# One decoder layer on one core: attention steps under a higher priority, the first x pairs on GpSimd's queue, sums tiles kept inside their group

## The chip, the core and the metric

The kernel runs on one core of one Trainium2 chip. The metric is the device time of one launch in microseconds (us). Of the kernel before, three runs took 2105.9, 2107.91 and 2104.35 us, so its median is 2105.9 us.

## What is computed

One layer for 256 tokens of width 2048, all in float32: a gated feed-forward block (f1), a mixing stage, cross-attention to 256 memory rows, a second feed-forward block (f2), a final norm. Cut to what matters:

```
h = x
h = h + 0.5 * swiglu(rmsnorm(h, g_ffn1), w1_gate, w1_up, w1_down)
z = rmsnorm(h, g_mix) @ w_in                      # u, v, q, k, v of the window attention
y_a = gelu(u) * (w_s @ rmsnorm(gelu(v)) + b_s)
y_b = window_attention_sinks(q, k, v, sinks)      # 16 heads of 64, window 128
h = h + concat(rmsnorm(y_a), rmsnorm(y_b)) @ w_out
h = h + cross_attention(rmsnorm(h, g_x), rmsnorm(mem, g_mem), w_xq, w_xkv, w_xo)
h = h + 0.5 * swiglu(rmsnorm(h, g_ffn2), w2_gate, w2_up, w2_down)
out = rmsnorm(h, g_final)
```

## The kernel before

**Products.** Every float32 operand is held as two float32r parts, a high part and what is left of it (names ending in h and l). `split` (L148 on ScalarE: a cast to the high part; L149 on VectorE: the subtraction that gives the low part) makes them from a value in float32, `split_scaled` (L142, L143) does it with a gain. A product is three matmuls: high by high, low by high, high by low (L363). Nearly all of TensorE's time is such 128x512 matmuls.

**Units and chunks.** A unit is a product of all 256 tokens by 1024 columns of a weight matrix, summed in up to seven PSUM banks that are named P, Q, R and so on behind the unit's name. It goes through its weights in chunks of 1 MB (`push`, `load`): the load is issued from SyncE (raw tile, three buffers), ScalarE casts wh, VectorE subtracts wl (two buffers each), TensorE multiplies. Where a chunk has kind S, VectorE also adds up sums of its blocks (t) and both engines split them into th and tl, of which there is one buffer each. In the names, f1gwh is the high part of a chunk of f1's gate and up weights, f1dwh and f1dth those of its down weights, uwh, vwh, mv0wh those of the mixing stage and of the memory's values. The token side of a product is a `Pair`: 256 rows of the transposed operand, split in the same way, plus split sums for kinds C and S. A pair of kind C needs half a tile of sums; two of them share a tile through the list `shared`.

**Order.** TensorE's order is the order of the program. The other engines' orders come from a scheduler, which picks among the instructions by priority (the place in the program; a `tc.high_priority()` block moves its instructions ahead) as dependencies and buffers become free in its own estimate. Once fixed, each engine works through its order one by one and waits at the first instruction that is not ready.

**Start.** The first unit (f1g, kind N) multiplies chunks c0, c1, c2 ... by the pairs n0 of x. The transposed x comes in pairs of 256 KB (n0r, L244, from SyncE's queue; the very first from ScalarE's). Beside it h (that is, x by rows) is loaded in four pieces of 512 KB (L747) and squared on ScalarE (junk, L138) for the norm. From c4 on, transposes of the scaled rows (n, L218) make the pairs n1 of the later units.

**Window attention** (`attend`, L861 and on) runs as side work between the matmuls of the units v, u and mv0, two lanes of it: scores (sc, TensorE), scaled, masked and maximum taken on VectorE (scs, mx, esk, nmx, L889 to L898), exponentials on ScalarE (L900), transposes on TensorE (pT), copied to SBUF by VectorE (pTs, L913), product with the values on TensorE (wop, L918), and the division at the end (esk L924, den L925, yb L928). In the same stretch the rows of memory are scaled into pairs mT for the unit mv0 (mTr L263, mTf, mTfh, mTfl; loads on GpSimd's queue), and ScalarE evacuates the units' banks through Gelu (v L956, u L969).

**Cross-attention** (`attend_memory`) is side work between the matmuls of xq and xo in the same way.

## Time and profile before

| | |
|---|---|
| three timed runs | 2104.35 to 2107.91 us, median 2105.9 us |
| the profiled execution | 2105.79 us by the timer, span 2104.0 us |
| outside the span | 1.79 us |
| TensorE busy | 2076.0 us, 99% of the span |
| VectorE, ScalarE, GpSimd busy | 1674.5, 1135.4, 32.2 us |
| mean granted TensorE clock | 0.996 |
| read from HBM | 398.52 MB, 190 GB/s over the span |

PE is TensorE, DVE VectorE, ACT ScalarE, POOL GpSimd, SP SyncE; PEclk is the clock that TensorE was granted, as a share of full speed. A row of a timeline has the start, the duration, engine, line, operation, output and inputs, and in brackets the idle time ahead of it with what ended it. On DVE and ACT the next instruction begins up to 0.1 us before the former's end in these rows.

### The profile page before, as it was taken

How to read it: one execution, taken by the hardware profiler on the slowest of the kernel's cores; microseconds unless marked ns; L12 is line 12 of the kernel's file. 1: busy time of each engine (PE TensorE's matmuls, PEld its weight loads, DVE VectorE, ACT ScalarE, POOL GpSimd, SP SyncE). 2: the span in 40 equal slices, each digit the busy share in tenths (PEclk: the TensorE clock that was granted, in tenths of full speed). 3: DMA queues.
4: the chain of work that ended last, by engine and by line, in shares of the span. 5: the costliest groups of instructions: out<-in, count | busy, mean ns of one | idle time of the engine just before them, and what ended most of it. 6: DMA issues, size and time to landing. Idle time of an engine off the chain costs nothing.

```text
span 2104.0 us, 23815 instructions
## 1 busy us (share of the span) xinstructions
PE 2076.0 (99%) x9527; PEld 1715.5 (82%) x9527; DVE 1674.5 (80%) x1609; ACT 1135.4 (54%) x1109; POOL 32.2 (2%) x51
## 2 busy tenths in 40 slices
PE   9999999999999999999999999999999999999998
PEld 7888888888888888788888888778888888888886
DVE  5888888888987745867858657798888888889878
ACT  7655555555544645544545455665555545555444
POOL 0000000000000000100000000000000000000000
PEclk9999999999999999999999999999999999999999
DMA  7555555555555554435555543455555555555553
GB/s 281 195 189 213 200 195 184 209 188 199 202 199 206 201 210 166 167 140 200 180 180 184 197 160 140 163 197 200 181 207 197 204 191 200 200 200 200 200 198 122
DMA packets 60110, 402.15 MB, mean 191 GB/s; under 512 B 6864, under 2 KB 8928, under 8 KB 12768
## 3 DMA queue, kind: packets, MB, share of 16 engines
q1 hardware_dynamic: 57280, 393.50, 51.7%
q0 software_dynamic: 2016, 6.30, 0.9%
q8 instruction: 74, 1.21, 0.2%
q10 hardware_dynamic: 704, 0.84, 0.1%
q14 instruction: 36, 0.29, 0.0%
HBM read 398.52 MB, written 2.10 MB: 190 GB/s over the span
## 4 chain that ended last, share of the span: by engine, by line
PE 94%; DVE 3%; ACT 1%; issue 1%; DMA 1%; POOL 0%; SPq 0%; POOLq 0%; DVEq 0%; ACTq 0%
PE f2gQ L363 16%; PE f1gQ L363 15%; PE f1dQ L363 6%; PE f2dQ L363 6%; PE f2gP L363 6%; PE f1gP L363 5%; PE f1dP L363 3%; PE f2dP L363 3%; PE woQ L363 2%; PE xqQ L363 2%; PE f1dR L363 2%; PE f2dR L363 2%; PE xoQ L363 2%; PE mk0Q L363 1%; PE mv1Q L363 1%; PE mv0Q L363 1%
## 5 line engine op out<-in xcount | busy, mean ns | idle before, releaser
L149 DVE TENSOR_TENSOR f1gwl<-f1gw,f1gwh 128x2048 fp32r<-128x2048 f32 (+1 forms) x91 | 185.5, 2043 | 51.6 <-ACT f1gwh L148 51.4
L148 ACT CAST f2gwh<-f2gw 128x1536 fp32r<-128x1536 f32 (+1 forms) x88 | 154.4, 1755 | 133.4 <-PE f2gQ L363 96.6
L148 ACT CAST f1gwh<-f1gw 128x2048 fp32r<-128x2048 f32 (+1 forms) x91 | 156.1, 1716 | 123.5 <-PE f1gQ L363 90.4
L149 DVE TENSOR_TENSOR f2gwl<-f2gw,f2gwh 128x1536 fp32r<-128x1536 f32 (+1 forms) x88 | 183.7, 2088 | 40.3 <-ACT f2gwh L148 40.2
L363 PE MATMUL f2gQ<-f2gwh,n4fh 128*128 128x512 f32 x363 | 141.4, 390 | 0.0
L363 PE MATMUL f2gQ<-f2gwh,n4fl 128*128 128x512 f32 x363 | 141.3, 389 | 0.0
L363 PE MATMUL f1gQ<-f1gwh,n1fh 128*128 128x512 f32 x330 | 128.6, 390 | 0.0
L363 PE MATMUL f1gQ<-f1gwh,n1fl 128*128 128x512 f32 x330 | 128.4, 389 | 0.0
L148 ACT CAST f2dwh<-f2dw 128x2048 fp32r<-128x2048 f32 (+1 forms) x44 | 79.2, 1799 | 91.2 <-PE f2dQ L363 71.2
L148 ACT CAST f1dwh<-f1dw 128x2048 fp32r<-128x2048 f32 (+1 forms) x44 | 79.2, 1799 | 87.9 <-PE f1dQ L363 68.2
L149 DVE TENSOR_TENSOR f2dwl<-f2dw,f2dwh 128x2048 fp32r<-128x2048 f32 (+1 forms) x44 | 94.4, 2145 | 27.0 <-ACT f2dwh L148 24.3
L363 PE MATMUL f2gQ<-f2gwl,n4fh 128*128 128x512 f32 x363 | 115.7, 392 | 0.0
L149 DVE TENSOR_TENSOR f1dwl<-f1dw,f1dwh 128x2048 fp32r<-128x2048 f32 (+1 forms) x44 | 94.3, 2144 | 26.8 <-ACT f1dwh L148 24.2
L363 PE MATMUL f1gQ<-f1gwl,n1fh 128*128 128x512 f32 x330 | 105.1, 392 | 0.0
L149 DVE TENSOR_TENSOR f2gtl<-f2gt,f2gth 128x2048 fp32r<-128x2048 f32 x33 | 75.6, 2292 | 17.0 <-ACT f2gth L148 16.6
L149 DVE TENSOR_TENSOR f1gtl<-f1gt,f1gth 128x2048 fp32r<-128x2048 f32 x30 | 68.8, 2292 | 18.3 <-ACT f1gth L148 18.0
L363 PEld LDWEIGHTS f2gQ<-f2gwh,n4fl 128*128 128x128 f32 x363 | 68.1, 188 | 14.2
L363 PEld LDWEIGHTS f2gQ<-f2gwh,n4fh 128*128 128x128 f32 x363 | 68.2, 188 | 14.1
L363 PEld LDWEIGHTS f2gQ<-f2gwl,n4fh 128*128 128x128 f32 x363 | 67.3, 188 | 13.5
L148 ACT CAST f2gth<-f2gt 128x2048 fp32r<-128x2048 f32 x33 | 63.1, 1913 | 23.1 <-DVE f2gt L314 18.3
L363 PEld LDWEIGHTS f1gQ<-f1gwh,n1fl 128*128 128x128 f32 x330 | 62.0, 188 | 12.9
L363 PEld LDWEIGHTS f1gQ<-f1gwh,n1fh 128*128 128x128 f32 x330 | 62.0, 188 | 12.8
(703 smaller groups left out, 5715.1 us busy)
## 6 DMA issues: line engine op xcount, KB each, us to landing
f2gw<-in_w_gu SPq DMA_DIRECT2D x88, 1024.0 KB, 4.8
f1gw<-in_w_gu SPq DMA_DIRECT2D x87, 1024.0 KB, 4.8
f1dw<-in_w_down SPq DMA_DIRECT2D x44, 1024.0 KB, 4.8
f2dw<-in_w_down SPq DMA_DIRECT2D x44, 1024.0 KB, 4.8
wow<-in_w_out SPq DMA_DIRECT2D x16, 1024.0 KB, 4.8
xqw<-in_w_xq SPq DMA_DIRECT2D x16, 1024.0 KB, 4.8
xow<-in_w_xo SPq DMA_DIRECT2D x16, 1024.0 KB, 4.8
qw<-in_w_in SPq DMA_DIRECT2D x8, 1024.0 KB, 5.0
```

Of the source, the lines that this page charges most:

```text
L148: nc.scalar.copy(hi, src)
L149: nc.vector.tensor_tensor(lo, src, hi.bitcast(F32), ALU.subtract)
L363: nc.tensor.matmul(self.banks[name], x, y, start=name not in self.begun, stop=self.left[name] == 0)
```

## The change

Three edits. First, in both attentions, steps on ScalarE and VectorE go under `tc.high_priority()`: in the window attention the mask, maximum and exponentials, the copy pTs and the division; in cross-attention the splits of the transposed queries, of the transposed probabilities and of the output, and the softmax. Second, the loads of the pairs of x (seven, 256 KB each) are issued by GpSimd instead of SyncE. Third, `shared` is emptied between groups of pairs (before mT and before n4), so that a C pair of mT does not take the other half of a sums tile that n1 opened, and one of n4 not that of mT.

```diff
-            nc.sync.dma_start(raw, srcT[i * T:(i + 1) * T, :].rearrange("(k p) t -> p k t", p=P))
+            nc.gpsimd.dma_start(raw, srcT[i * T:(i + 1) * T, :].rearrange("(k p) t -> p k t", p=P))
...
     mT = []
+    shared.clear()
...
-                sc = s2("scs")
...
-                nc.vector.scalar_tensor_tensor(
-                    out=sv, in0=pv, scalar=0.125, in1=bnd, op0=ALU.mult, op1=ALU.add
-                )
...
+                with tc.high_priority():
+                    sc = s2("scs")
...
+                    nc.vector.scalar_tensor_tensor(
+                        out=sv, in0=pv, scalar=0.125, in1=bnd, op0=ALU.mult, op1=ALU.add
+                    )
...
-                pts = s2("pTs")
-                nc.vector.tensor_copy(pts, pt)
+                with tc.high_priority():
+                    pts = s2("pTs")
+                    nc.vector.tensor_copy(pts, pt)
...
-            nc.scalar.activation(esk, esk, AF.Exp)
-            nc.vector.tensor_tensor(den, den, esk, ALU.add)
-            nc.vector.reciprocal(den, den)
...
+            with tc.high_priority():
+                nc.scalar.activation(esk, esk, AF.Exp)
+                nc.vector.tensor_tensor(den, den, esk, ALU.add)
+                nc.vector.reciprocal(den, den)
...
-            split(qh[:, 2 * half:2 * half + 2, :], ql[:, 2 * half:2 * half + 2, :], pv)
+            with tc.high_priority():
+                split(qh[:, 2 * half:2 * half + 2, :], ql[:, 2 * half:2 * half + 2, :], pv)
...
-        split(ph, pl, ptv)
+        with tc.high_priority():
+            split(ph, pl, ptv)
...
+    shared.clear()
     n4, on4, rs4_ = next_norm("n4", G_FFN2, KINDS)
```

TensorE's order of instructions is the same in both programs. The other engines' orders differ at five stretches. In the first feed-forward block's first unit, ScalarE and VectorE both change. On ScalarE, n0r_143 is the second pair of x and n0h_122 its high part, for chunk c1, whose cast is f1gwh_150; junk are the squares of h; the rows stand between the casts of c0 and of c2:

```order
 L148 CAST f1gwh_129<-f1gw_128 128x512 x3
-L142 ACTIVATE n0h_122<-n0r_143,sm 128x256 x2
 L148 CAST f1gwh_150<-f1gw_149 128x2048
-L142 ACTIVATE n0h_183<-n0r_185,sm 128x256 x2
 L138 ACTIVATE junk_192,parts_120<-h 128x512
 L138 ACTIVATE junk_194,parts_120<-h 128x512
+L142 ACTIVATE n0h_122<-n0r_143,sm 128x256 x2
+L142 ACTIVATE n0h_183<-n0r_185,sm 128x256 x2
 L138 ACTIVATE junk_197,parts_120<-h 128x512
```

The pair for c1 has moved behind c1's cast and behind two squares of h. On VectorE its low part n0l has likewise moved from ahead of c1's f1gwl to right behind it; and before chunk c5's pair, two more n1fl subtractions stand ahead of the subtraction f1gwl of c6, behind which n0l for c5 stays.

In f1's down projection, near 620 us of the trace, VectorE's order of the low parts has changed. f1dtl_4469 is the low part of a chunk's sums, f1dwl_4515 that of the chunk behind it, the f1afl are low parts of pairs of activations:

```order
 L313 TENSOR_TENSOR f1dt_4467<-f1dt_4467,f1dw_4463 128x512
+L149 TENSOR_TENSOR f1afl_4545<-f1a_3244,f1afh_4544 128x512
+L149 TENSOR_TENSOR f1dwl_4465<-f1dw_4463,f1dwh_4464 128x1536
 L314 TENSOR_TENSOR f1dt_4467<-f1dt_4467,f1dw_4463 128x512
-L149 TENSOR_TENSOR f1dwl_4465<-f1dw_4463,f1dwh_4464 128x1536
-L149 TENSOR_TENSOR f1afl_4545<-f1a_3244,f1afh_4544 128x512
+L149 TENSOR_TENSOR f1afl_4588<-f1a_3244,f1afh_4587 128x512
+L149 TENSOR_TENSOR f1dwl_4515<-f1dw_4513,f1dwh_4514 128x2048
 L149 TENSOR_TENSOR f1dtl_4469<-f1dt_4467,f1dth_4468 128x2048
-L149 TENSOR_TENSOR f1dwl_4515<-f1dw_4513,f1dwh_4514 128x2048
```

The sums' low part now comes behind that of the next chunk and one more f1afl. On ScalarE the casts f1dth and the next chunk's f1dwh have changed places in the same way, and both orders repeat this at the next chunk of kind S, near 630 us.

In the unit u, near 845 us, VectorE's order ahead of one copy pTs is this before (mTf, mTfl and n1fl belong to the memory pairs; n1fl there is a half tile of sums that n1 opened; uwl_6230 is the low part of u's third chunk):

```order
L960 SCALAR_TENSOR_TENSOR v_5731<-v_5731,rs_6103,gv_5729 128x1024
L960 SCALAR_TENSOR_TENSOR v_5732<-v_5732,rs_6103,gv_5729 128x1024
L263 SCALAR_TENSOR_TENSOR mTr_6110<-mTr_6110,sm,by_token 128x2x128 x2
L198 TENSOR_TENSOR mTf_6117<-mTr_6110 128x256
L149 TENSOR_TENSOR uwl_6230<-uw_6228,uwh_6229 128x2048
L149 TENSOR_TENSOR mTfl_6116<-mTr_6110,mTfh_6115 128x512
L149 TENSOR_TENSOR n1fl_632<-mTf_6117,n1fh_631 128x256
L263 SCALAR_TENSOR_TENSOR mTr_6129<-mTr_6129,sm,by_token 128x2x128 x2
L198 TENSOR_TENSOR mTf_6138<-mTr_6129 128x256
L913 COPY pTs_6165<-pT_6160 128x512
```

And this now:

```order
L964 SCALAR_TENSOR_TENSOR v_5731<-v_5731,rs_6103,gv_5729 128x1024
L964 SCALAR_TENSOR_TENSOR v_5732<-v_5732,rs_6103,gv_5729 128x1024
L932 TENSOR_TENSOR yb_5723<-wop_5810,den_5811 128x512
L263 SCALAR_TENSOR_TENSOR mTr_6110<-mTr_6110,sm,by_token 128x2x128 x2
L149 TENSOR_TENSOR uwl_6146<-uw_6144,uwh_6145 128x2048
L198 TENSOR_TENSOR mTf_6119<-mTr_6110 128x256
L149 TENSOR_TENSOR mTfl_6116<-mTr_6110,mTfh_6115 128x512
L149 TENSOR_TENSOR mTfl_6118<-mTf_6119,mTfh_6117 128x256
L149 TENSOR_TENSOR uwl_6230<-uw_6228,uwh_6229 128x2048
L263 SCALAR_TENSOR_TENSOR mTr_6131<-mTr_6131,sm,by_token 128x2x128 x2
L198 TENSOR_TENSOR mTf_6138<-mTr_6131 128x256
L916 COPY pTs_6165<-pT_6160 128x512
```

Behind v's scaling and ahead of pTs there now stand two rows more, the division yb and the low part uwl_6146 of u's second chunk, which stood ahead of v's scaling before; pTs has kept its place in the queue. On ScalarE the exponential of esk has moved ahead of v's Gelu, with one table load for it, and the cast of u's second chunk has moved behind the four squares of v.

Behind the unit u, where mv0 begins (near 895 us), ScalarE's order has an exponential between u's second and third evacuation, and with it two table loads (ACT_TABLE_LOAD) more. In cross-attention the maximum xmx has moved ahead of one subtraction each of the queries' and the keys' split. From there on the orders of all engines are the same.

## The prediction

> **What bounds the kernel now.** The page comes first, for which engine is full; then the windows by stage, for where that engine is not; then the waits of TensorE, for what it misses there.

> ```profile
> span 2104.0 us, 23815 instructions
> PE 2076.0 (99%) x9527; PEld 1715.5 (82%) x9527; DVE 1674.5 (80%) x1609; ACT 1135.4 (54%) x1109; POOL 32.2 (2%) x51
> ```

> TensorE is idle for 2104.0 - 2076.0 = 28.0 us in all, and its order does not change. Below, a window's columns are its length, busy time of PE, PEld, DVE, ACT and POOL, granted clock, DMA share and GB/s.

> ```profile
> 0.00:62.00 62.00, 57.25 (x247) 45.28 (x248) 38.06 (x54) 46.60 (x81) 2.97 (x12) 0.97 0.75 269
> 820.00:860.00 40.00, 35.43 (x159) 28.63 (x158) 26.10 (x42) 24.28 (x46) 6.51 (x9) 0.91 0.37 132
> ```
> ```profile
> 36.00:46.00 10.00, 7.54 (x30) 5.66 (x28) 6.98 (x11) 5.40 (x10) 0.00 (x0) 0.83 0.81 286
> 845.00:858.00 13.00, 8.43 (x27) 6.25 (x26) 9.96 (x20) 5.08 (x12) 2.88 (x4) 0.74 0.36 121
> ```
> ```profile
> PE wop L918 <- DVE pTs L913: 4.8, 2, 4.6
> ```

> The start and the attention near 850 us hold 4.75 + 4.57 = 9.3 us of the idle time, and the clock falls in both: 10 x (1 - 0.83) = 1.7 us of full speed are lost in one, 13 x (1 - 0.74) = 3.4 us in the other. What this change can win lies there, about 14 us; anything that makes TensorE wait elsewhere is lost in full, since TensorE has no other work.

> **The start, x from GpSimd's queue: +1.1 us.** Chunk c1 began so:

> ```profile
> 11.91 1.91 ACT L148 CAST f1gwh<-f1gw 128x2048 fp32r<-128x2048 f32 x1 [1.66 <-DMA f1gw<-in_w_gu]
> 13.72 0.90 ACT L142 ACTIVATE n0h<-n0r,sm 128x256 fp32r<-128x256 f32 x2
> 14.53 0.62 ACT L138 ACTIVATE junk<-h 128x512 f32<-128x512 f32 x1
> ```
> ```profile
> 13.85 2.29 DVE L149 TENSOR_TENSOR f1gwl<-f1gw,f1gwh 128x2048 fp32r<-128x2048 f32 x1 [3.07 <-ACT f1gwh L148]
> ```
> ```profile
> 13.87 0.50 PE L363 MATMUL f1gP<-f1gwh,n0h 128*128 128x512 f32 x1 [0.62 <-ACT f1gwh L148]
> ...
> 14.68 0.40 PE L363 MATMUL f1gP<-f1gwh,n0l 128*128 128x512 f32 x1
> ...
> 19.86 0.50 PE L363 MATMUL f1gP<-f1gwh,n0h 128*128 128x512 f32 x1 [0.22 <-ACT f1gwh L148]
> ...
> 25.86 0.50 PE L363 MATMUL f1gP<-f1gwh,n0h 128*128 128x512 f32 x1 [0.25 <-ACT f1gwh L148]
> ```
> ```profile
> 5.30 1.71 SPq L747 DMA_DIRECT2D h<-in_x  x2
> ```
> ```profile
> h<-in_x SPq DMA_DIRECT2D x1, 512.0 KB, 8.6
> ```

> c1's pair was ready before its weights. Now ScalarE first squares two pieces of h, and the first h, issued at 5.30, lands 8.6 us later, at 13.9 (the last row is that one load). So: two squares of 0.62 to 15.1; n0h's halves, 0.45 each (row of 13.72), at 15.6 and 16.0; VectorE, through with f1gwl at 16.1, makes n0l's halves by 16.5. c1's fourth matmul moves from 14.68 to some 16.5, by 1.85. The waits of 0.22 and 0.25 us ahead of c2 and c3 (19.86, 25.86) are for weights and absorb 0.47; 1.4 reaches c5.

> c5 waited before, and still does:

> ```profile
> 35.78 0.39 PE L363 MATMUL f1gQ<-f1gwh,n0l 128*128 128x512 f32 x1
> ...
> 38.58 0.50 PE L363 MATMUL f1gP<-f1gwh,n0h 128*128 128x512 f32 x1 [0.59 <-ACT n0h L142]
> 40.95 0.79 PE L363 MATMUL f1gP<-f1gwh,n0l 128*128 128x512 f32 x1 [1.87 <-DVE n0l L143]
> ```
> ```profile
> 38.21 2.29 DVE L149 TENSOR_TENSOR f1gwl<-f1gw,f1gwh 128x2048 fp32r<-128x2048 f32 x1
> 40.41 0.88 DVE L143 SCALAR_TENSOR_TENSOR n0l<-n0r,sm,n0h 128x256 fp32r<-128x256 f32 x2
> ```

> n0l stays behind the subtraction of c6's weights, whose cast needs the buffer that the matmul of 35.78 reads last. That one is 1.4 late, so the cast runs from 37.6 to 39.4, f1gwl to 41.6, n0l's first half to 42.05: 1.1 later than 40.95. From there TensorE runs through as before (c7's pair, earlier than now, was no wait). The start costs +1.1 us, with -0.5 (a piece of h that lands earlier, since two pairs no longer lie ahead of it in its queue) and +2.7 (it lands 1.3 later, below) as ends. The issues themselves cost nothing: GpSimd does little then, and SyncE is relieved of seven.

> ```profile
> n0r<-in_xT SPq DMA_DIRECT2D x6, 256.0 KB, 7.1
> ...
> snk<-in_sinks POOLq DMA_DIRECT2D x1, 8.0 KB, 5.1
> ```

> GpSimd's one load there took 5.1 us for 8 KB, SyncE's pairs 7.1 for 256 KB, so a pair issued near 3.4 lands by about 10.5 at worst, far ahead of 15.1. [...]

> **The sums' order in f1's down projection: +1.8 us.** No intent of the change, only a consequence of tiles that come free at other times.

> ```profile
> 616.99 1.92 ACT L148 CAST f1dth<-f1dt 128x2048 fp32r<-128x2048 f32 x1
> 618.90 1.92 ACT L148 CAST f1dwh<-f1dw 128x2048 fp32r<-128x2048 f32 x1
> ...
> 630.15 1.91 ACT L148 CAST f1dwh<-f1dw 128x2048 fp32r<-128x2048 f32 x1
> ```
> ```profile
> 619.14 2.28 DVE L149 TENSOR_TENSOR f1dtl<-f1dt,f1dth 128x2048 fp32r<-128x2048 f32 x1
> ```
> ```profile
> 618.43 0.39 PE L363 MATMUL f1dQ<-f1dwh,f1afl 128*128 128x512 f32 x1
> ...
> 624.33 1.07 PE L363 MATMUL f1dQ<-f1dtl,f1afh 128*128 128x512 f32 x4
> ...
> 628.63 0.39 PE L363 MATMUL f1dQ<-f1dwh,f1afl 128*128 128x512 f32 x1
> ...
> 634.53 1.07 PE L363 MATMUL f1dQ<-f1dtl,f1afh 128*128 128x512 f32 x4
> ```

> f1dtl was ready at 621.4 and used at 624.33, a margin of 2.9. Now the next chunk's cast goes first. It began at 618.90 right behind f1dth; it writes a buffer that TensorE reads last with the matmul of 618.43 (0.39), so it cannot begin before 618.8, and f1dwl follows from 620.8 to 623.0, f1dtl from 623.0 to 625.25: TensorE waits 0.9 us. The next S chunk, 0.9 late, repeats it: the cast of 630.15 waits for the matmul of 628.63, over at 629.0 + 0.9 = 629.9, and ends at 631.8, f1dth follows to 633.7, VectorE does f1dwl from 631.9 and f1dtl from 634.1 to 636.3; TensorE wants it at 634.53 + 0.95 = 635.5: 0.85 more. Together +1.8; the ends are 0 (the cast finds its buffer free by 2 us more than I count) and 2.3. Near 550 and 560 us the same shuffle leaves margins of over 2.5 us.

> **The urgent steps near 850 us: -0.4 us.**

> ```profile
> 834.79 1.90 ACT L148 CAST uwh<-uw 128x2048 fp32r<-128x2048 f32 x1
> ...
> 837.91 1.28 ACT L924 ACT_TABLE_LOAD   x1
> ```
> ```profile
> 838.94 0.68 DVE L928 TENSOR_TENSOR yb<-wop,den 128x512 f32<-128x512 f32 x1
> ...
> 841.26 2.48 DVE L960 SCALAR_TENSOR_TENSOR v<-v,rs,gv 128x1024 f32<-128x1024 f32 x2 [0.84 <-POOL rs L133]
> ...
> 849.30 0.68 DVE L913 COPY pTs<-pT 128x512 f32<-128x512 f32 x1
> ```

> pTs waits not for its transposes but for its turn: from v's scaling to pTs VectorE is busy without a gap. With the cast of 834.79 (1.8) and the table load of 837.91 (1.28) moved out of the squares' way, v's scaling starts about 3.2 us earlier, at 838.1. But the subtraction uwl (2.2) and yb (0.6) now come behind it and ahead of pTs: 3.2 - 2.8 = 0.4 gained, the wait stays at 4.2 of 4.57, and the low clock with it.

> **At nothing.** The two table loads more near 895 us cost ScalarE 2 x 1.28 and hold up u's third bank; when it was read, and when mv0R wants it:

> ```profile
> 898.43 0.69 ACT L969 ACTIVATE u<-uR,rs 128x512 f32<-128x512 f32 x1 [0.38 <-PE uR L363]
> ```
> ```profile
> 905.24 0.48 PE L363 MATMUL mv0R<-mv0wh,mTfh 128*128 128x512 f32 x1
> ```

> Even 3.5 us later (2 x 1.28 and an exponential with its wait) it is read by 902.7, so 2.5 us of other banks' matmuls cover it; without that cover it would cost up to 3. The steps in cross-attention move by one subtraction or two (0.6 to 1.2 us) where TensorE did not wait, and the sums tiles cost no instruction.

> **The sum** against the profiled execution: 2105.8 + 1.1 + 1.8 - 0.4 = 2108.3 us; that execution lies 0.1 below the median of the three runs, so no correction is due.

> **The rivals.** Slower for good: the squares of h hold c1 for longer. This stage runs its loads so (the second column from the right is the DMA engines' share):

> ```profile
> 12.00:26.00 14.00, 12.92 (x55) 9.71 (x54) 6.66 (x9) 12.35 (x24) 0.73 (x1) 1.00 1.04 403
> ```

> If pairs three and four (512 KB; at 403 GB/s 1.3 us) go ahead of h, n0h starts at 16.4; TensorE then idles near 4 us and the clock falls there as well, by the price of the window at 36 us, 1.7. 2108.3 + 1.3 + 1.7 = 2111.3. It decides from a landing of h later than about 14.8. For it: the pairs no longer wait in SyncE's queue. Against it: their buffers are few.

> The change does what it says at 850 us: pTs comes right behind its transposes, the wait of 4.57 and the 3.4 us of clock go, 2108.3 + 0.4 - 8.0 = 2100.7. Against it stands VectorE's order, in which pTs keeps its place.

> The orders change nothing that TensorE feels: h early, f1dtl in time, pTs 0.4 earlier: 2105.4.

> The clock falls elsewhere. In the trace the low clock follows an idle stretch of 2.4 us near 40 us (1.7 lost) and of 4.6 near 850 (3.4 lost); both stretches move by some tenths. If neither triggers it, 2108.3 - 5.1 = 2103.2. [...]

> **How the numbers follow.** My forecast, 2106.4 to 2110, has 0.45; the slower rival 0.25; no effect 0.12; the clock 0.08; the stall at 850 gone 0.10. A difference of 0.2%, 4.2 us, is about what a measurement of this kernel can tell from none: faster means below 2101.7, slower above 2110.1. Faster: 0.10 and a little of the clock's rival, 0.12. Slower: 0.25 and the forecast's upper edge, 0.27. Same: 0.61. The range, 2102.5 to 2111.8, leaves out the stall's end and the tails.

> **What would show it.** Right: c1's first matmuls wait for ACT n0h and DVE n0l with idle time near 2.5 us; PE f1dQ waits for DVE f1dtl twice in the 620s and 630s, 0.9 us each; wop still waits over 4 us for pTs with the clock near 0.74. Wrong: if wop's wait is gone, the queue's order was not the reason; if f1dQ does not wait, the casts were not held by their buffers; if PE is idle near 895 to 910, the table loads were not covered.

## The result and the profile after

The changed kernel took 2113.0 us (median of 7 runs, 2112.07 to 2114.26), the kernel before 2105.9 (7 runs, 2104.35 to 2107.91): 1.0034 times as long, with a 95% interval of 1.0022 to 1.0045. That is 7.1 us more, where 2.4 were forecast. The profiled execution of after took 2113.46 us, 0.5 above its median; its page begins so:

```profile
span 2111.7 us, 23799 instructions
PE 2078.7 (98%) x9527; PEld 1716.9 (81%) x9527; DVE 1673.5 (79%) x1609; ACT 1138.0 (54%) x1111; POOL 37.2 (2%) x58
```

TensorE is idle for 33.0 us, 5.0 more than before, and busy for 2.7 more with the same matmuls: that part is clock (0.50 for 17.1 us up to 2080 us, in before for 10.2). The windows by stage (length, busy time of PE, PEld, DVE, ACT, POOL, granted clock, DMA share, GB/s), first of after, then of before for the two stages that the prediction does not show:

```profile
0.00:62.00 62.00, 53.89 (x233) 42.96 (x234) 36.41 (x51) 46.20 (x79) 7.96 (x19) 0.94 0.70 256
820.00:860.00 40.00, 35.98 (x171) 29.38 (x170) 27.40 (x49) 22.43 (x47) 6.51 (x9) 0.94 0.43 158
880.00:920.00 40.00, 39.52 (x204) 32.32 (x203) 29.55 (x57) 26.57 (x42) 2.88 (x4) 1.00 0.43 153
1310.00:1335.00 25.00, 23.30 (x122) 19.95 (x121) 16.73 (x24) 13.54 (x24) 0.00 (x0) 0.93 0.23 85
```
```profile
880.00:920.00 40.00, 40.00 (x210) 33.55 (x209) 31.98 (x58) 23.48 (x37) 1.44 (x2) 1.00 0.40 140
1310.00:1335.00 25.00, 23.30 (x126) 19.84 (x125) 14.84 (x20) 13.05 (x20) 0.00 (x0) 1.00 0.34 123
```

In the start TensorE works 3.4 us less than before (57.25), at a clock of 0.94 instead of 0.97. Near 900 us TensorE idles, where it did not. Near 1320 us it is as busy as before (23.30 us of 25), but at a clock of 0.93 instead of 1.00. Of the waits of TensorE after, these are new or have changed (us in total, times, the longest):

```profile
PE f1gP L363 <- ACT n0h L142: 5.0, 3, 3.2
PE wop L921 <- DVE pTs L916: 4.0, 1, 4.0
...
PE f1dQ L363 <- DVE f1dtl L149: 1.2, 2, 0.6
...
PE sv L1001 <- DVE pTs L916: 0.3, 1, 0.3
PE sv L1001 <- DVE u L1008: 0.2, 1, 0.2
PE xs L153 <- DVE mkh L149: 0.2, 1, 0.2
```

Since TensorE's order did not change, every matmul has its counterpart, and the difference of the two starts says how late TensorE is at that place. Rows of after, at c1, at c5, at both ends of f1's down projection and of mv0's first chunk:

```profile
16.52 0.51 PE L363 MATMUL f1gP<-f1gwh,n0h 128*128 128x512 f32 x1 [3.20 <-ACT n0h L142]
40.88 0.49 PE L363 MATMUL f1gP<-f1gwh,n0h 128*128 128x512 f32 x1 [0.95 <-ACT n0h L142]
621.47 0.39 PE L363 MATMUL f1dQ<-f1dwh,f1afl 128*128 128x512 f32 x1
639.75 1.20 PE L363 MATMUL f1dQ<-f1dtl,f1afh 128*128 128x512 f32 x4 [0.60 <-DVE f1dtl L149]
909.55 0.48 PE L363 MATMUL mv0R<-mv0wh,mTfh 128*128 128x512 f32 x1
919.19 0.47 PE L363 MATMUL mv0Q<-mv0wh,mTfh 128*128 128x512 f32 x1
```

The last of them in before was this:

```profile
913.88 0.47 PE L363 MATMUL mv0Q<-mv0wh,mTfh 128*128 128x512 f32 x1
```

Against 13.87, 38.58, 618.43, 634.53 and 905.24 of before (rows in the prediction) and 913.88 they are late by 2.65, 2.30, 3.04, 5.22, 4.31 and 5.31 us; the span by 7.7. So the start costs 3.0, the down projection 2.2, 0.9 comes back up to mv0 (1.1 in the attention, less 0.2 lost before it), mv0's first chunk costs 1.0. Of the last 2.4, 0.5 stands at the wait for mkh and 1.5 near 1320 us, where the clock was low (0.50) for one stretch of 3.4 us; 0.4 lies behind the last matmul.

One execution further down, that of urgent_pts_only, was granted 0.85 of the clock nearly from end to end; its time is not compared.

### The profile page after: what moved, and what is told of

Read it like the earlier page. It is cut to its first block, busy times and chain, and to the rows that moved or that the text cites. A ratio compares the mean times of both kernels' runs of the same rounds, so it can differ in the third digit from the quotient of the medians.

```text
span 2111.7 us, 23799 instructions
## 1 busy us (share of the span) xinstructions
PE 2078.7 (98%) x9527; PEld 1716.9 (81%) x9527; DVE 1673.5 (79%) x1609; ACT 1138.0 (54%) x1111; POOL 37.2 (2%) x58
## 4 chain that ended last, share of the span: by engine, by line
PE 92%; DVE 4%; ACT 2%; DMA 1%; issue 1%; POOL 0%; SPq 0%; POOLq 0%; DVEq 0%; ACTq 0%
PE f2gQ L363 16%; PE f1gQ L363 15%; PE f2dQ L363 6%; PE f1dQ L363 6%; PE f2gP L363 6%; PE f1gP L363 5%; PE f2dP L363 3%; PE f1dP L363 3%; PE woQ L363 2%; PE xqQ L363 2%; PE f2dR L363 2%; PE xoQ L363 2%; PE f1dR L363 2%; PE mk0Q L363 1%; PE mv1Q L363 1%; PE mk1Q L363 1%
## 5 line engine op out<-in xcount | busy, mean ns | idle before, releaser
L149 DVE TENSOR_TENSOR f1gwl<-f1gw,f1gwh 128x2048 fp32r<-128x2048 f32 (+1 forms) x91 | 185.8, 2042 | 59.3 <-ACT f1gwh L148 59.1
L148 ACT CAST f1gwh<-f1gw 128x2048 fp32r<-128x2048 f32 (+1 forms) x91 | 156.0, 1715 | 132.5 <-PE f1gQ L363 94.0
L148 ACT CAST f2gwh<-f2gw 128x1536 fp32r<-128x1536 f32 (+1 forms) x88 | 154.3, 1753 | 133.5 <-PE f2gQ L363 96.4
L149 DVE TENSOR_TENSOR f2gwl<-f2gw,f2gwh 128x1536 fp32r<-128x1536 f32 (+1 forms) x88 | 183.6, 2088 | 40.3 <-ACT f2gwh L148 40.3
L363 PE MATMUL f2gQ<-f2gwh,n4fh 128*128 128x512 f32 x363 | 141.4, 390 | 0.0
L363 PE MATMUL f2gQ<-f2gwh,n4fl 128*128 128x512 f32 x363 | 141.3, 389 | 0.0
L148 ACT CAST f1dwh<-f1dw 128x2048 fp32r<-128x2048 f32 (+1 forms) x44 | 79.1, 1798 | 92.0 <-PE f1dQ L363 71.7
L363 PE MATMUL f1gQ<-f1gwh,n1fh 128*128 128x512 f32 x330 | 128.6, 390 | 0.0
L363 PE MATMUL f1gQ<-f1gwh,n1fl 128*128 128x512 f32 x330 | 128.4, 389 | 0.0
L148 ACT CAST f2dwh<-f2dw 128x2048 fp32r<-128x2048 f32 (+1 forms) x44 | 79.1, 1798 | 91.0 <-PE f2dQ L363 72.9
L149 DVE TENSOR_TENSOR f1dwl<-f1dw,f1dwh 128x2048 fp32r<-128x2048 f32 (+1 forms) x44 | 94.3, 2144 | 29.9 <-ACT f1dwh L148 27.5
L363 PE MATMUL f2gQ<-f2gwl,n4fh 128*128 128x512 f32 x363 | 115.7, 392 | 0.0
L149 DVE TENSOR_TENSOR f2dwl<-f2dw,f2dwh 128x2048 fp32r<-128x2048 f32 (+1 forms) x44 | 94.3, 2144 | 26.6 <-ACT f2dwh L148 24.0
L363 PE MATMUL f1gQ<-f1gwl,n1fh 128*128 128x512 f32 x330 | 105.1, 392 | 0.0
L149 DVE TENSOR_TENSOR f2gtl<-f2gt,f2gth 128x2048 fp32r<-128x2048 f32 x33 | 75.6, 2292 | 17.0 <-ACT f2gth L148 16.5
L149 DVE TENSOR_TENSOR f1gtl<-f1gt,f1gth 128x2048 fp32r<-128x2048 f32 x30 | 68.8, 2292 | 15.4 <-ACT f1gth L148 15.0
L363 PEld LDWEIGHTS f2gQ<-f2gwh,n4fl 128*128 128x128 f32 x363 | 68.1, 188 | 14.2
L363 PEld LDWEIGHTS f2gQ<-f2gwh,n4fh 128*128 128x128 f32 x363 | 68.1, 188 | 14.1
L363 PEld LDWEIGHTS f2gQ<-f2gwl,n4fh 128*128 128x128 f32 x363 | 67.3, 188 | 13.5
L148 ACT CAST f2gth<-f2gt 128x2048 fp32r<-128x2048 f32 x33 | 63.1, 1911 | 23.1 <-DVE f2gt L314 18.3
L363 PEld LDWEIGHTS f1gQ<-f1gwh,n1fl 128*128 128x128 f32 x330 | 62.0, 188 | 12.9
L363 PEld LDWEIGHTS f1gQ<-f1gwh,n1fh 128*128 128x128 f32 x330 | 61.9, 188 | 12.8
```

What stands on the lines that cost most here:

```text
L148: nc.scalar.copy(hi, src)
L149: nc.vector.tensor_tensor(lo, src, hi.bitcast(F32), ALU.subtract)
L363: nc.tensor.matmul(self.banks[name], x, y, start=name not in self.begun, stop=self.left[name] == 0)
```

## The experiments

Each kernel was timed beside the kernel before, whose medians lie between 2105.78 and 2105.93 us. A ratio is known to 0.001 (2 us), so smaller differences are read in the traces. In the expectations, "chunk 5's casts" are the two casts on ScalarE near 36 to 39 us: that of the weights behind chunk 5 (the prediction's c6) and that of chunk 5's pair.

| kernel | median us | ratio to before, 95% |
|---|---|---|
| x_alone | 2109.14 | 1.0018, 1.0009 to 1.0027 |
| urgent_alone | 2106.28 | 1.0001, 0.9992 to 1.0009 |
| clear_alone | 2108.91 | 1.0016, 1.0007 to 1.0025 |
| x_pair1_first | 2107.99 | 1.0013, 1.0004 to 1.0022 |
| x_chunk5_order | 2110.39 | 1.0019, 1.0010 to 1.0028 |
| x_both_orders | 2106.80 | 1.0005, 0.9996 to 1.0014 |
| clear_sums_first | 2106.64 | 1.0007, 0.9998 to 1.0016 |
| after_two_orders_back | 2111.53 | 1.0026, 1.0016 to 1.0036 |
| after_all_orders_back | 2108.44 | 1.0013, 1.0004 to 1.0022 |
| pts_scalar | 2106.49 | 1.0005, 0.9996 to 1.0014 |
| urgent_scores_only | 2105.89 | 1.0000, 0.9991 to 1.0009 |
| memory_later | 2099.27 | 0.9967, 0.9955 to 0.9980 |
| memory_later_pair5_first | 2096.85 | 0.9957, 0.9945 to 0.9969 |

### One edit at a time

x_alone is the kernel before with the first line of this, clear_alone with the second (at both places), urgent_alone with all the urgent blocks:

```diff
-            nc.sync.dma_start(raw, srcT[i * T:(i + 1) * T, :].rearrange("(k p) t -> p k t", p=P))
+            nc.gpsimd.dma_start(raw, srcT[i * T:(i + 1) * T, :].rearrange("(k p) t -> p k t", p=P))
...
+    shared.clear()
...
+                with tc.high_priority():
...
```

> Before, with only the loads of x's pairs moved to GpSimd's queue. By the prediction's reckoning the start costs +1.1 us (2107.0 us) and nothing else moves. By the reading of the two traces the whole of the start comes back: chunk 1's first matmul 2.6 us later, because ScalarE takes h's two squares ahead of pair 1's casts and the first weight chunk and h land later, and a second window of half clock near 45 us, about +3.0 us in all (2109 us). A rival: the start alone costs less than that, and the rest of the 2.6 us came from another edit (2106 to 2107 us).

> Before, with only the steps of both attentions marked urgent. By the prediction: -0.4 us near 850 us and nothing at the memory values' first chunk or in the cross-attention (2105.5 us). By the reading of the traces: -1.05 us near 850 and 877 us, +0.96 us at the memory values' first chunk, +0.37 us in the cross-attention, so +0.3 us (2106.2 us); with the 1.6 us of a half-clock window near 1317 us on top if that window belongs to this edit (2107.8 us), without it if the window comes by the phase of the clock's windows.

> Before, with only the list of shared tiles of sums emptied before the memory's and before the down projection's pairs. By the prediction +1.8 us (2107.7 us), all of it at the first chunks of the first down projection; by the traces +2.0 to +2.2 us there. A rival: without the later start the sums are not late there, and nothing moves (2105.9 us).

By the medians the edits cost 3.35, 0.5 and 3.1 us, and their sum, 7.0, is close to the change's 7.1. Each of the three is known to 2 us only, and the profiled executions differ in where the clock was low, so the close agreement is partly chance; that the edits do not act on one another is not shown by it. In x_alone c1 began at 16.62 and the clock fell there (this execution, 2110.93 us, was the slowest of its eleven). The two rows are a stretch of 3.4 us and the 6.8 behind it:

```profile
12.39:15.81 3.42, 0.98 (x5) 0.48 (x3) 1.51 (x1) 2.86 (x4) 0.00 (x0) 1.00 1.07 395
15.81:22.64 6.83, 6.02 (x14) 4.63 (x15) 4.29 (x6) 6.83 (x17) 0.72 (x1) 0.50 1.03 407
```

The trace of urgent_alone has the gain of 1.1 and the losses of 0.97 and 0.45 us at the three places that the expectation names, and full clock near 1320 us; a third stretch of half clock near 855 us, where before had two, takes 0.8 of the gain back (0.995 granted over that execution, 0.996 over that of before). In clear_alone the two waits for f1dtl are there (1.2 us in all) though nothing was late before them, which rules out the rival; its trace puts 2.2 us into the down projection, as in after, and the rest of its 3.1 is a third stretch of half clock near 855 us (0.995 granted).

### The start: which order, or the loads

x_pair1_first puts pair 1 ahead again on both engines, with the loads as in x_alone: h's squares and the split of c1's weights are ordered behind the steps of pair 1 (`paired` holds, for each pair of x, the ScalarE and the VectorE instruction of its second half).

```diff
                 for tb in range(TB):
-                    square_into(parts1[:, tb, j:j + 1], hj[:, tb, :], 512)
+                    with tc.issue_after(paired[1][0].ins):
+                        square_into(parts1[:, tb, j:j + 1], hj[:, tb, :], 512)
...
             nc.sync.dma_start(raw, w)
-            split(wh, wl, raw)
+            with ExitStack() as behind:
+                if s == "f1g" and len(paired) == 2:
+                    for ins in paired[1]:
+                        behind.enter_context(tc.issue_after(ins.ins))
+                split(wh, wl, raw)
```

x_chunk5_order puts back the other place where x_alone's order differs, near 36 us, and x_both_orders does both:

```diff
         if kind != "N":
-            fill(s, p, raw)
+            with ExitStack() as behind:
+                if s == "n1":
                    held_back.append(p)
                if s == "n1" and len(held_back) == 2:
+                    for ins in paired[5]:
+                        behind.enter_context(tc.issue_after(ins.ins))
+                fill(s, p, raw)
```

> x_alone, with pair 1's casts and subtractions put ahead of chunk 1's cast and of h's squares on ScalarE and VectorE; the loads stay as in x_alone. If the order on ScalarE and VectorE is the cause of the late start, chunk 1's first matmul comes at about 14.4 us instead of 16.5 and only the 0.5 us of the later first chunk stays: start +0.5 to +1 us (2106.5 us). If the loads themselves are the cause (h, the weights and the pairs share the transfer engines from two queues), chunk 1 still starts after 16 us, or chunk 2 takes over the delay at 22.5 us, and it stays at +3 us (2109 us).

> x_alone, with one order put back as before on ScalarE and VectorE: the second pair of n1 is split behind pair 5 of x, so chunk 5's casts (near 36 us) go ahead of it again; chunk 1 stays late as in x_alone. If the lasting delay of the start comes from that order at chunk 5 and the late chunk 1 is swallowed by the waits ahead of chunks 2, 3 and 5, then chunk 1 still begins near 16.5 us, chunk 5 near 38.6 to 39.2 instead of 41 to 43, and the time is 2106 to 2107 us. If the late chunk 1 itself is what lasts (the prediction's step), chunk 5 begins at 40 us or later and the time stays near 2109.

> x_alone, with both orders of the start put back on ScalarE and VectorE: pair 1 ahead of chunk 1's cast and of h's squares, and chunk 5's casts ahead of the second pair of n1. The loads stay on GpSimd's queue. If the two orders are the whole cost, each by itself enough to make the start late, chunk 1 begins near 14.2 us, chunk 5 near 39 us, no more than one window of half clock comes near 42 us, and the time is 2106 to 2106.8 us. If the loads have a price of their own (w1 and h land later), 1 us or more stays: 2107 us or above.

TensorE's rows at c1 and c5 in x_pair1_first, then at c5 in x_chunk5_order and in x_both_orders:

```profile
14.20 0.50 PE L370 MATMUL f1gP<-f1gwh,n0h 128*128 128x512 f32 x1 [0.95 <-ACT f1gwh L148]
...
40.90 0.50 PE L370 MATMUL f1gP<-f1gwh,n0h 128*128 128x512 f32 x1 [2.02 <-ACT n0h L142]
```
```profile
42.65 0.50 PE L373 MATMUL f1gP<-f1gwh,n0h 128*128 128x512 f32 x1 [0.59 <-ACT n0h L142]
```
```profile
39.64 0.50 PE L377 MATMUL f1gP<-f1gwh,n0h 128*128 128x512 f32 x1 [0.84 <-ACT n0h L142]
```

With pair 1 ahead c1 begins at 14.20, as the expectation has it if the order is the cause, and c5 at 40.90 all the same, exactly where after has it (40.88). What fixes it there is ScalarE's order ahead of c5. The same stretch on ScalarE before and after:

```profile
32.07 0.84 ACT L236 ACTIVATE n1r<-n,sm 128x256 f32<-128x256 f32 x2
...
36.21 1.91 ACT L148 CAST f1gwh<-f1gw 128x2048 fp32r<-128x2048 f32 x1
38.02 0.90 ACT L142 ACTIVATE n0h<-n0r,sm 128x256 fp32r<-128x256 f32 x2
```
```profile
34.47 0.83 ACT L236 ACTIVATE n1r<-n,sm 128x256 f32<-128x256 f32 x2
...
37.27 0.41 ACT L148 CAST n1fh<-n1f 128x256 fp32r<-128x256 f32 x1 [0.57 <-DVE n1f L198]
37.58 0.62 ACT L148 CAST n1fh<-n1r 128x512 fp32r<-128x512 f32 x1
38.21 0.41 ACT L148 CAST n1fh<-n1f 128x256 fp32r<-128x256 f32 x1
38.52 1.90 ACT L148 CAST f1gwh<-f1gw 128x2048 fp32r<-128x2048 f32 x1
40.33 1.70 ACT L142 ACTIVATE n0h<-n0r,sm 128x256 fp32r<-128x256 f32 x4
```

Two casts of n1 (37.58 and 38.21, 0.94 us) have gone ahead of the weights' cast and of n0h, with them a wait of 0.57 for VectorE's n1f, and n1r has gone behind the cast of the chunk before (0.8): 40.33 - 38.02 = 2.31, and c5 is 2.30 late. But x_chunk5_order alone, which puts back the two casts, does not help either: its c5 begins at 42.65, because the stall at c1 had brought half clock from 15.19 to 22.02 in that execution and TensorE itself was 4 us late. Each order is enough to lose the start: in after, where c1 brought no half clock, 2.1 us of its delay were still there behind c3's wait (27.93 against 25.86). With both back (x_both_orders) c1 begins at 14.21 and c5 at 39.64, 0.34 and 1.06 late, n1r's place not being restored, and the median is 0.9 above before. That leaves 0.9 us as the loads' own price, with up to 2.9 inside the interval; its trace can't settle it, since that execution had no half clock near 42 us (1.00 from 36 to 46), where before had 3.4 us of it.

### f1's down projection

```diff
-            split(th, tl, t)
+            sums[:] = split(th, tl, t)
...
+                if s == "f1d":
+                    for ins in sums:
+                        behind.enter_context(tc.issue_after(ins.ins))
                 split(wh, wl, raw)
```

> clear_alone, with the cast and the subtraction of a chunk's sums put ahead of those of the next chunk in the first down projection, the only two casts and three subtractions that move. If the prediction's step is right (the next chunk's cast is held by its buffer and holds the sums up), the two waits of TensorE for f1dtl go, and with them 1.7 to 2.1 us: 2106 to 2107 us. If the waits have another cause, they stay and the time is 2108.9 as in clear_alone.

Two casts and the subtractions behind them moved, and the waits for f1dtl fell from 1.2 us to this:

```profile
PE f1dQ L368 <- DVE f1dtl L148: 0.2, 1, 0.2
```

The median came down by 2.3 us. In the traces 1.6 of the 2.2 us are gone and 0.6 stay, at the second chunk; the two profiled executions differ besides by the clock near 42 us (1.00 from 39.50 to 46.32 in this one). The rows of after show the order that the prediction gave, the next chunk's cast ahead of the sums'. It let that cast begin at 618.8; with the 3.04 us of the start that is 621.84:

```profile
621.90 1.91 ACT L148 CAST f1dwh<-f1dw 128x2048 fp32r<-128x2048 f32 x1 [1.85 <-PE f1dQ L363]
623.72 1.91 ACT L148 CAST f1dth<-f1dt 128x2048 fp32r<-128x2048 f32 x1
```

### The changed kernel with its orders put back

after_two_orders_back is the changed kernel with the edits of x_chunk5_order and clear_sums_first, after_all_orders_back has that of x_pair1_first too.

> The changed kernel with both orders put back: chunk 5's casts ahead of the second pair of n1 in the start, the sums ahead of the next chunk's weights in the first down projection. All three edits stay. If these two orders are what the change costs, 2113.0 - 2.3 (start) - 1.9 (down projection) = 2108.8 us, and less by what the second half-clock window at the start cost, 1.7: 2107 to 2109 us. If other costs of the edits weigh more, it stays above 2110.

> The changed kernel with all three orders put back: chunk 1's pair, chunk 5's casts, the sums of the first down projection. All three edits stay. If the orders are what the change costs, 2105.9 + 0.4 (w1 lands later) + 0.5 (what urgent_alone measured) = 2106.8 us; if they are not, 2109 us or more.

With c1 still late the time is 2111.5 us (the trace has half clock at c1 and near 1320 us, 0.994 granted); with all three orders back it is 2108.4, of 7.1 us 4.6 undone. That is 1.6 more than was expected. In its profiled execution (2110.06, the slowest of eleven, 0.994 granted) the rest is there as 1.2 at c5, 1.0 for a second stretch of half clock behind it and 0.7 for a third near 855 us, 0.6 in the down projection, 1.0 at mv0 and 0.5 in cross-attention, less 1.1 in the attention. By the medians all three edits are still 2.5 us slower than none, with 0.8 to 4.6 in the interval.

### The stall near 850 us

The change marked pTs urgent, and its wait only fell from 4.57 to 4.02 us; the fall is not even pTs's own, for urgent_scores_only (below), where pTs is not urgent, has 4.01. Two attempts to take pTs out of VectorE's queue, first pts_scalar, then memory_later:

```diff
-                nc.vector.tensor_copy(pts, pt)
+                nc.scalar.copy(pts, pt)
```
```diff
-    pu = unit("u", w_in, 0, n2, lambda i: mT.append(pair_normalized("mT", KINDS[i], memT, i, G_MEM, by_token)))
+    def memory_pair(i):
+        mT.append(pair_normalized("mT", KINDS[i], memT, i, G_MEM, by_token))
+
+    pu = unit("u", w_in, 0, n2, lambda i: memory_pair(i - 1) if i else None)
+    memory_pair(len(KINDS) - 1)
```

> Before, with one edit: the copy of the transposed weights (pTs) out of its bank is made on ScalarE instead of VectorE. If the 4.6 us wait near 850 us is VectorE's queue, as the prediction said, and not the transposes, it goes, the half clock behind it (3.4 us or more) goes too, and the time is 2105.9 - 4.6 - 3.4 = 2098 us. If the wait is for something else (po's bank, the vector steps that follow), the time stays within 2104 to 2106.

> Before, with one edit: each pair of the normalized memory is built one chunk of u's unit later, so that on VectorE 4.7 us of other work (a weights subtraction of 2.3, a pair's scaling and subtractions) no longer stand between v's scaling and the pTs that TensorE waits for near 850 us. If that wait is VectorE's queue, it falls from 4.6 us to under 1 and the half clock behind it (two or three windows, 3.4 to 5.1 us of lost work) goes as well: 2105.9 - 4 - 3.4 = 2098.5 us. If the wait is for something else, it stays, and the time is within 2104 to 2107. A rival: the memory's pairs now come late for mv0 and TensorE waits there instead.

pts_scalar left the wait (4.79 us, now for ScalarE), and its rows say why that tells nothing of the cause: on ScalarE the copy stands behind two casts that wait for VectorE's mTr.

```profile
848.73 0.62 ACT L148 CAST mTfh<-mTr 128x512 fp32r<-128x512 f32 x1 [4.02 <-DVE mTr L263]
849.26 0.40 ACT L148 CAST mTfh<-mTf 128x256 fp32r<-128x256 f32 x1
849.56 0.58 ACT L913 COPY pTs<-pT 128x512 f32<-128x512 f32 x1
```

In memory_later only one pair's scaling stands between v's scaling and pTs on VectorE. Its rows, TensorE's, and the window that showed 8.43 us of work and a clock of 0.74 before:

```profile
841.44 2.48 DVE L960 SCALAR_TENSOR_TENSOR v<-v,rs,gv 128x1024 f32<-128x1024 f32 x2 [0.84 <-POOL rs L133]
843.84 0.88 DVE L263 SCALAR_TENSOR_TENSOR mTr<-mTr,sm,by_token 128x256 f32<-128x256 f32 x2
...
845.09 0.68 DVE L913 COPY pTs<-pT 128x512 f32<-128x512 f32 x1
```
```profile
845.83 1.10 PE L918 MATMUL wop<-kv,pTs 128*128 128x64 f32 x8 [0.17 <-DVE pTs L913]
```
```profile
845.00:858.00 13.00, 12.83 (x61) 10.19 (x61) 12.46 (x20) 7.58 (x14) 2.88 (x4) 1.00 0.45 153
```

The wait is 0.17, the clock 1.00, the time 6.7 us below before; a new wait of 1.0 for the exponentials near 861 us takes some back. The stall was VectorE's queue, and a later place of the filler in the program removed what the priority had only shortened.

The same kernel with one more order, against the wait at c5 that before had already:

```diff
+                if s == "f1g" and len(paired) == 7:
+                    for ins in paired[5]:
+                        behind.enter_context(tc.issue_after(ins.ins))
                 split(wh, wl, raw)
```

> memory_later, with one more order: in the start the cast and the subtraction of chunk 6's weights go behind those of pair 5 of x, so that chunk 5's pair no longer stands behind a weights subtraction of 2.3 us on VectorE. If chunk 5's two waits (0.6 and 1.9 us near 38.6 and 41 us) are that order, they go, and with them the window of half clock near 41 us, 1.7: 2099.3 - 2.4 - 1.7 = 2095.2 us; 2096.9 if the window stays. If pair 5 is late for another reason (its load, the pairs of n1), the waits stay: 2099.

```profile
36.00:46.00 10.00, 8.67 (x41) 6.63 (x40) 9.10 (x16) 8.61 (x17) 0.00 (x0) 1.00 0.66 227
```

Of the waits of 0.59 and 1.87, 0.66 and 0.68 are left: n0l came 1.2 us earlier, n0h no earlier. The low clock (0.83 before) is gone in this execution (1.00); in those of clear_sums_first and x_both_orders it is gone too, with the whole wait in place, so it can't all be put down to the edit. The gain is 2.4 us of the 4.1 hoped for, and 2096.85 us is the fastest kernel here, 8.9 below before.

### The memory values' first chunk

urgent_pts_only is before with only this block, urgent_scores_only is urgent_alone without it:

```diff
-                pts = s2("pTs")
-                nc.vector.tensor_copy(pts, pt)
+                with tc.high_priority():
+                    pts = s2("pTs")
+                    nc.vector.tensor_copy(pts, pt)
```

> Before, with only the copy pTs marked urgent, not the scores' steps and exponentials. If the two waits of TensorE at the memory values' first chunk (0.45 and 0.51 us) come from the exponentials and table loads that ScalarE takes ahead of mv0's casts, they are not there; if they come from pTs, they are. The wait near 850 us stays over 4 us by either.

> urgent_alone, with the copy pTs no longer marked urgent; the scores' steps, the exponentials and the steps of cross-attention stay so. On ScalarE the exponentials near 900 us then stand behind mv0's second cast again, without the two extra table loads. If the waits of TensorE at the memory values' first chunk (0.45 and 0.51 us, for sv's bank and for pTs) come from that order, they go here; if they come from the urgent scores on VectorE, they stay. The time is 2105 to 2106.5 us in both cases, so the trace decides, not the time.

urgent_pts_only had no such wait, but TensorE ran at 0.85, and other waits of it were shorter in that execution too (0.3 us in all for f1gwh where before has 1.1, 0.7 for f2dtl where before has 1.2): it decides nothing. urgent_scores_only has no wait for sv either, with the two extra table loads gone and mv0's cast back ahead of the exponentials; its wait for mkh in cross-attention (0.2 us) stayed. In after the cast stands behind three table loads:

```profile
902.08 1.28 ACT L902 ACT_TABLE_LOAD   x1
...
904.00 1.28 ACT L973 ACT_TABLE_LOAD   x1
...
906.58 1.28 ACT L902 ACT_TABLE_LOAD   x1
...
909.66 1.90 ACT L148 CAST mv0wh<-mv0w 128x2048 fp32r<-128x2048 f32 x1
```
```profile
915.34 2.28 DVE L149 TENSOR_TENSOR mv0wl<-mv0w,mv0wh 128x2048 fp32r<-128x2048 f32 x1
917.54 0.68 DVE L916 COPY pTs<-pT 128x512 f32<-128x512 f32 x1
```
```profile
918.28 1.16 PE L1001 MATMUL sv<-v,wst 128*128 128x128 f32 x8 [0.26 <-DVE pTs L916]
```

The late casts make VectorE's subtractions late, pTs comes behind one of them, and TensorE waits for the bank that pTs has yet to empty. urgent_scores_only put back two things at once, ScalarE's order and pTs's place on VectorE. pts_scalar parts them: nothing in it is urgent, yet its ScalarE takes the same three table loads (898.67, 900.59, 903.67) with mv0's cast behind them (906.46), and TensorE has the first of the two waits, 0.21 us for u at 912.07. So that one goes with the table loads and not with any priority; that the second follows from them through pTs is read from after's rows alone.

## Why the prediction was wrong, point by point

**The start: the step that failed most, +1.1 forecast, 3.0 in the trace and 3.35 alone.** "1.4 reaches c5", where the pair is "1.1 later than 40.95" behind c6's subtraction: c5 is late by 2.3, and it would be so without a late c1, because n1's casts went ahead on ScalarE: in x_pair1_first c1 is 0.34 late and c5 2.32. The front part had named the n1 subtractions that moved; the prediction let c7's pair pass as "no wait" and did not count the casts that went with them. And c1 was mis-sized: its fourth matmul came 3.0 late (17.69 against 14.68), not 1.85. By the prediction's own steps 16.5 is when the second matmul has its n0l; the fourth comes 0.5 behind it. The rest is loads: w1's cast began at 12.45 instead of 11.91, and the first square of h at 14.73, when h had landed, where the prediction has 13.9. Both ScalarE rows are these, first w1's cast, then the squares of h:

```profile
12.45 1.90 ACT L148 CAST f1gwh<-f1gw 128x2048 fp32r<-128x2048 f32 x1 [3.16 <-DMA f1gw<-in_w_gu]
14.73 0.63 ACT L138 ACTIVATE junk<-h 128x512 f32<-128x512 f32 x1 [0.38 <-DMA h<-in_x]
```

Both loads had been issued earlier than before, w1 by 0.5 and h by 2.2 us, and landed later all the same. c3's pair, issued at 7.90 on GpSimd's queue, landed at 14.51, ahead of h and w2, which SyncE had issued at 3.13 and 5.30; before, issued at 7.80 on SyncE's queue, it landed at 18.54. By what rule a load of one queue passes those of another no run shows. The rival "slower for good" set its point at a landing of h later than 14.8 and priced low clock at c1 with 1.7; h landed 0.1 short of it, and x_alone and x_chunk5_order did show the low clock there (0.50 from 15.81 and from 15.19 us). It had the better mechanism for c1, though one pair passed h, not two. The forecast's upper end for the start, +2.7 for an h that lands 1.3 later, is not worked out there (1.1 and 1.3 make 2.4), and no run shows such an h; c5 was 2.3 late with an h 0.8 later, and the low clock behind it (0.50 from 42.43 to 49.26) made that 3.0.

**The down projection, +1.8: right.** 2.2 in the trace, 1.1 at each of the two chunks it named (0.6 of it shown as idle), f1dtl ready at 628.33 where 625.25 + 3.04 = 628.29, and putting the two casts back takes 1.6 off in the trace.

**The attention near 850 us, -0.4: right in cause, short in sum.** pTs gained 0.5 and its wait stayed 4.02 of 4.57; the queue was the cause (memory_later). A second, short wait near 877 us went as well, which gave 0.5 and which the prediction did not look for. The 838.1 at which it had v's scaling start holds to 0.1: 843.43 in after, where TensorE is 5.4 late.

**"At nothing": wrong at both places.** The table loads near 895 us were priced through u's third bank ("read by 902.7"), and that was covered; what was late instead is mv0's cast behind them, then two subtractions, then pTs and u: 1.0 us. The cross-attention's step cost 0.5.

**The clock: not in the sum.** The forecast kept the clock as it was. In the profiled execution of after it was low (0.50) for 6.8 us near 45 (3.4 before) and for 3.4 near 1320 us: some 2.7 us of the 7.7 by TensorE's longer busy time. The first is part of the start's 3.0: c5 is 2.3 late, the chunks behind it 3.0. The latter need not come from an edit: its waits, 0.68 and 1.02 us, are the same in before, and pts_scalar, which changes nothing there, has the half clock too (0.50 from 1317.10 to 1320.52), while after_all_orders_back, with all three edits, has not.

Had the prediction had 3.0 for the start, 2.2, -0.9 and 1.5 for the rest, it would have stood at 2111.6; the clock near 1320 us, 1.5, makes up most of what remains to the 2113.46 of the profiled execution.

## What to carry to other kernels

An edit that frees a scheduler to reorder is priced by all that it lets pass ahead, engine by engine, and not by the moved step alone: each order that cost time here was a filler (squares of h, casts of n1, the next chunk's weights, table loads) that slipped ahead of the one cast that TensorE wanted next. Where TensorE is 99% busy, first ask of each engine's queue what stands ahead of what TensorE waits for; deferring that filler by one chunk gave 6.7 us where a higher priority gave 0.5 at that wait. And price a wait with the clock that it may cost: behind the 4.57 us near 850 us of before TensorE ran at 0.50 for 6.8 us.

## What the runs showed of the hardware

```profile
1319.02:1322.43 3.41, 1.71 (x7) 1.05 (x7) 2.38 (x3) 0.59 (x1) 0.00 (x0) 1.00 0.33 96
1322.43:1325.85 3.42, 3.42 (x15) 3.23 (x15) 0.00 (x0) 0.12 (x1) 0.00 (x0) 0.50 0.52 216
```
```profile
1314.06:1317.47 3.41, 2.29 (x11) 1.76 (x12) 1.56 (x3) 0.04 (x1) 0.00 (x0) 1.00 0.53 183
```

c1's wait of 3.25 us in x_alone was followed by half clock, that of 3.20 in after was not: in x_alone one stretch had 2.4 us without a matmul, in after two had 1.8 and 1.5. The waits of 4.57 us (before) and 4.02 (after) near 850 each left one stretch with no matmul at all. Executions of before with a mean granted clock of 0.997 took 2104.20 to 2104.73 us, those with 0.994 2107.52 to 2107.94; that the place of the grid makes this difference is an estimate from these figures, and no run tests it.

**Loads from GpSimd.** The issue of a pair of x took 0.72 to 0.76 us on GpSimd where SyncE took 0.37 to 0.43, and the pair landed 6.6 us after it where it was 6.7 before (medians of 7 pairs). It is the others that landed later: w1 0.5 us and h's first piece 0.8, though they had been issued 0.5 and 2.2 us earlier.
